# Softmax probabilities copied by DMA and transposed as float32r in whole groups; rotary half copies issued by SyncE

## The chip, the core and the metric

The kernel runs on one core of a Trainium2 chip. Time is device time in microseconds (us) for one execution, the median of several runs. A profile of one execution is read beside it. The engines are PE (TensorE: matmuls, with its weight loads as PEld), DVE (VectorE), ACT (ScalarE), POOL (GpSimd) and SP (SyncE, which only issues DMAs here). Each runs its own queue of instructions in order, and they wait for each other by semaphores.

## The reference

Two layers of a flow-matching backbone over 512 latent tokens and 256 context tokens, model width 1024, in float32. Each layer normalises and modulates its input, projects it into three groups of eight attention heads (width 64) and a gate, attends, and projects back:

```python
hx = rmsnorm(x, norm_w) * (1 + scale[:, None, :]) + shift[:, None, :]
px = split_cols(hx @ w_in)
ya, yca = global_gqa(px[0], px[1], px[2], ...)          # A: all latent and context keys, rotary
yb, ycb = neighbourhood_attn(px[3], px[4], px[5], ...)  # B: 8 x 16 window on a grid, bias, context keys
yc_, ycc = window_gqa(px[6], px[7], px[8], ...)         # C: +-128 tokens, rotary, sink, context keys
ux = jnp.concatenate([ya, yb, yc_], axis=-1) * jax.nn.silu(px[9])
x = x + gate[:, None, :] * (ux @ w_out)
```

Every group is a softmax over scores and a weighted sum of values:

```python
p = softmax_f32(s, v_all.dtype)
return jnp.einsum('bhgqk,bkhd->bqhgd', p, v_all)
```

In the first layer the context tokens go through the same weights and attend to themselves; the second layer computes latent tokens alone.

## The kernel before

**Numbers.** Most matmuls run in float32r, whose precision is not enough alone, so each operand is split into a high part (a rounded copy, made by ACT) and a low part (the rest, by DVE or POOL), and products are summed from two or three such pairs. A weight block is loaded to `ws` by SP (L251 and L497), rounded to `wh` (L242) and subtracted to `wl` (L245).

**Attention.** For a head, `scores` multiplies a tile of 128 queries with the keys into PSUM (`Sbig`); DVE takes the row maximum (`negm`, in B and C with the mask added on the way into `P`); ACT writes the exponentials into an SBUF tile `P` of 128 rows and up to 768 columns, in float32, and sums the rows. `values` needs P with the keys on the partitions, so PE transposes it, 128 x 128 at a time, into a PSUM bank `T` (2 buffers): `turn`, L1031, a matmul in transpose mode with the P block as the stationary operand and the identity as the moving one. The bank is a group: the blocks of two to four query tiles for one key block (B and C), or four blocks of two tiles (A and the context). `pt_copy` splits T into `pth` (ACT) and `ptl` (DVE), and `pv` (L1028) multiplies both with the values `vt` into `Obig`. There are four passes over P per pair of heads in A (two tiles of queries each), two in B and C (four tiles each), and two more for the context queries in the first layer. `o_out` (L1043) then adds the upper and the lower half of `Obig` into `OT`: ACT copies rows 64 to 128 to a scratch tile `otmp`, DVE adds rows 0 to 64 to it.

P has five buffers (`P=5` in CFG, L51).

**Rotary of C.** In `rope_c` (L945) the four 32-row bands of q are swapped by four DMAs of 64 KB from SBUF to SBUF (`tB<-tA`, L958), issued by ACT; POOL multiplies and adds.

**Order.** The program is written as generators that interleave one pair's attention with the next pair's projection. The order that counts is made by a planner, `arrange`: it builds a graph of all instructions, with buffers and PSUM banks, gives each instruction a cost (`Step.cost`) and lays the engines' queues out by list scheduling in several passes; the result is fixed as the order of each engine's queue, SP's included. Its costs are numbers in the code; for PE 108 ns for a float32 transpose, for a DMA 330 ns of SP or 260 of another queue, and then 2550 ns plus the bytes at 395 a ns until it has landed.

Of the kernel before, what the change touches and what calls it, by code (L numbers as in the profile page):

```python
# [20 lines left out]
D = 1024  # L21
# [29 lines left out]
CFG = dict(hp=600, hpf=600, pj=2, T=2, O=1, P=5, qt=5, kt=4, vt=4, gt=3, wh=5, ws=3, pt=3, bm=2, tA=1, OT=1, u=1, tl=1, turns=6, ab="pj", tR=1, map={}, ada=2, h0=300, h1=1000, a0=9, H=2, hr=0, cp="A", cv="A", w0="D", w1="D", w2=(("D", "D"), ("D", "D")), hb="D", ws_="P")  # L51
# [700 lines left out]
def mixers(tc, nc, l, last, p1, ps, const, env):  # L752
# [192 lines left out]
    def rope_c(s, scale, need_ctx, bank):  # L945
# [11 lines left out]
        for b in range(4):  # L957
            nc.scalar.dma_start(sw[b * 32:(b + 1) * 32], q[(b ^ 1) * 32:((b ^ 1) + 1) * 32])  # L958
# [70 lines left out]

    def turn(*args, **kw):  # L1030
        return nc.tensor.transpose(*args, **kw)  # L1031
# [12 lines left out]
    def o_out(O, OT, h, c0, n):  # L1044
        tmp = p1.tile([64, 512], F32, name="otmp", bufs=1)
        nc.scalar.activation(tmp[:, 0:n], O[64:128, 0:n], AF.Copy)  # L1046
        nc.vector.tensor_add(OT[64 * h:64 * h + 64, c0:c0 + n], O[0:64, 0:n], tmp[:, 0:n])  # L1047
# [39 lines left out]
    class CtxUnit(Unit):  # L1087
        def scores(self):
# [11 lines left out]
            self.P = newP()  # L1100
            for t in range(2):
                nc.scalar.activation(self.P[:, t * 256:(t + 1) * 256], S[:, t * 256:(t + 1) * 256], AF.Exp,
                                     bias=self.stat("negm", 4 + t), accum_out=self.stat("sums", 4 + t))
            yield 0.45

        def values(self):
            T = psT()
            for kb in range(2):
                for t in range(2):
                    turn(T[:, (2 * kb + t) * 128:(2 * kb + t + 1) * 128],  # L1110
                                        self.P[:, t * 256 + kb * 128:t * 256 + (kb + 1) * 128], ident)
# [8 lines left out]
    class GlobalUnit(Unit):  # L1120
        def scores(self):
# [8 lines left out]
            for i in self.tiles:  # L1130
# [5 lines left out]
                self.P.append(P)  # L1136
                yield 0

        def values(self):
            O = half_O()  # L1140

            def turns(k2):
                T = psT()
                for k in range(2):
                    for j in range(2):

                        o = ((k2 + k + 2) % 6 if j else k2 + k) * 128
                        turn(T[:, (2 * k + j) * 128:(2 * k + j + 1) * 128], self.P[j][:, o:o + 128], ident)
                return pt_copy(T, 512)

            def sums(k2, pt):
                for k in range(2):
                    pv(O, self.v(k2 + k), pt, k * 256, 0, 256, k2 + k == 0, k2 + k == 5)

            yield from ahead([(lambda k2=k2: turns(k2), lambda pt, k2=k2: sums(k2, pt), 0.45) for k2 in range(0, 6, 2)])
# [4 lines left out]
    class BandUnit(Unit):  # L1160
        def scores(self):
# [3 lines left out]
            for pair in ((1, 2), (0, 3)):  # L1165
# [11 lines left out]
                for i in pair:  # L1177
# [10 lines left out]
                    self.P[i] = P  # L1188
# [20 lines left out]
    class NearUnit(Unit):  # L1209
# [9 lines left out]
        def scores(self):  # L1219
            self.P = {}  # L1220
            for i in (1, 2, 0, 3):
# [22 lines left out]
                self.P[i] = P  # L1244
                yield 0

        def values(self):
            O = psO()
            for n, kb in enumerate((4, 5, 1, 2, 3, 0)):
                qs = [i for i in range(4) if kb in self.PLAN[i][4]]  # L1250
                T = psT()
                for j, i in enumerate(qs):
                    o = self.PLAN[i][4][kb]
                    turn(T[:, j * 128:(j + 1) * 128], self.P[i][:, o:o + 128], ident)
# [276 lines left out]
    def urgent(gen):  # L1531
        while True:
# [12 lines left out]
            T=CFG["T"], spr=2, nw=1, P=CFG["P"], qt=CFG["qt"], kt=CFG["kt"], vt=CFG["vt"], gt=CFG["gt"], negm=2,  # L1545
            bm=CFG["bm"], sums=2, pth=CFG["pt"], ptl=CFG["pt"], rec=2, ssA=2, qd=2, qs=2, ex=2, xr=3, xn0=8, room=9,
# [3 lines left out]
TO_PE, TO_OTHER, FIXED, RATE = 400.0, 150.0, 2550.0, 395.0  # L1550
WAIT = {"PE": 53.0, "POOL": 78.0, "ACT": 36.0, "DVE": 36.0, "SP": 30.0}
# [14 lines left out]
class Step:  # L1566
# [16 lines left out]
    def cost(self):  # L1583
# [6 lines left out]
        self.plain = False  # L1590
        if self.dma:
            b = 4 * outs[0][2][0][1] * size(outs[0][2])
            self.busy = 330.0 if e == "SP" else 260.0
            self.move = 3460.0 if stem(outs[0][0].name) == "bc" else b / RATE
        elif e == "PE":
            n = size(ins[0][2])
            self.exact = ins[0][4] == "float32"
            self.busy = (108.0 if n == 128 else 230.0) if self.exact else max(n / 2.4 + 13.5, 66.0)
            self.last = 272.0 if self.exact else n / 2.4 + 180.0
# [34 lines left out]
class Graph:  # L1634


    def __init__(self, steps, tiles, needed):
# [37 lines left out]
        for a, b in needed:  # L1675
            self.before[at[a]].setdefault(at[b], 0)
        self.users = {name: u for name, u in users.items() if name in tiles and not tiles[name][1]}
# [287 lines left out]
```

## Time and profile before

| | |
|---|---|
| Median of 3 runs | 1178.56 us (1177.38 to 1178.78) |
| The profiled execution | 1178.53 us, its span 1176.3 us, mean granted clock 0.996 |
| Instructions profiled | 21720 |
| DMA | 124.21 MB, mean 106 GB/s |
| Costliest groups on PE | L329 `pj<-wh,hL` 189.2 us, L308 `pj<-hL,wh` 186.4 us, L1031 `T<-ident,P` 177.9 us |

The page gives busy time by engine, the span in slices, DMA queues, the chain of work that ended last, and groups of instructions by line, `out<-in`. Matmuls are pipelined, so their durations overlap; what one costs is read from the distance between starts in the timeline. A group's row ends with the idle time of its engine ahead of it and what ended that.

### The profile page before, as it was taken

The numbers are of one execution on the slowest core, as the hardware profiler recorded it, in microseconds if no ns is written. First come the engines' busy times: TensorE is split into PE (matmuls) and PEld (weight loads), VectorE is DVE, ScalarE is ACT, GpSimd is POOL, SyncE is SP. The second block draws the span as 40 slices with busy tenths as digits, with TensorE's granted clock in tenths as the row PEclk, the third lists the DMA queues.
The fourth block names the chain that finished last, engine by engine and source line by source line (L and its number), as shares of the span: only waits on it lengthen the run. The fifth ranks groups of instructions, "written<-read, shape, count | busy, mean of one in ns | idle before, by whom it ended". The sixth has DMA issues, their size and how long they took to land. (4 is left out here: it accounts for less than half of the span.)

```text
span 1176.3 us, 21720 instructions
## 1 busy us (share of the span) xinstructions
PE 1141.1 (97%) x8016; PEld 1028.0 (87%) x8016; DVE 766.3 (65%) x1548; ACT 697.8 (59%) x1581; POOL 401.7 (34%) x496
## 2 busy tenths in 40 slices
PE   5999999999999999999999999999999999999996
PEld 3799989998898898988788999989988989898885
DVE  5667666665455665657979855676665566668652
ACT  5447555566557666678723634555656677778641
POOL 2442111125445456367300030221235665466001
PEclk9999999999999999999999999999999999999998
DMA  9633222213222222122577432233221121123152
GB/s 359 209 99 99 83 70 95 101 55 112 81 69 96 72 77 86 59 64 91 157 253 265 153 129 88 88 98 98 88 79 60 58 72 53 57 63 108 37 170 72
DMA packets 60825, 124.21 MB, mean 106 GB/s; under 512 B 7216, under 2 KB 13488, under 8 KB 60720
## 3 DMA queue, kind: packets, MB, share of 16 engines
q1 hardware_dynamic: 54768, 111.96, 29.8%
q10 hardware_dynamic: 5952, 10.88, 2.8%
q8 instruction: 63, 1.03, 0.4%
q14 instruction: 42, 0.34, 0.1%
HBM read 109.05 MB, written 11.14 MB: 102 GB/s over the span
## 5 line engine op out<-in xcount | busy, mean ns | idle before, releaser
L1024 DVE TENSOR_TENSOR ptl<-T,pth 128x512 fp32r<-128x512 f32 (+2 forms) x312 | 181.4, 591 | 119.3 <-ACT pth L778 114.7
L778 ACT ACTIVATE pth<-T 128x512 fp32r<-128x512 f32 (+2 forms) x312 | 160.7, 522 | 103.5 <-PE T L1031 93.1
L329 PE MATMUL pj<-wh,hL 128*128 128x256 f32 x896 | 189.2, 289 | 0.2 <-DVE vt L854 0.2
L308 PE MATMUL pj<-hL,wh 128*128 128x512 f32 x544 | 186.4, 405 | 0.0
L1031 PE MATMUL T<-ident,P 128*128 128x128 f32 x1024 | 177.9, 274 | 5.7 <-DVE ptl L1024 2.8
L1028 PE MATMUL Sbig<-kt,qt 128*128 128x256 f32 (+1 forms) x864 | 162.0, 309 | 1.2 <-DVE negm L1240 0.8
L242 ACT ACTIVATE wh<-ws 128x512 fp32r<-128x512 f32 x192 | 120.2, 630 | 67.3 <-PE pj L308 16.2
L1031 PEld LDWEIGHTS T<-ident,P 128*128 128x128 f32 x1024 | 124.8, 140 | 29.3 <-DVE ptl L1024 8.1
L329 PEld LDWEIGHTS pj<-wh,hL 128*128 128x128 f32 x896 | 147.3, 190 | 2.1 <-issue 1.3
L245 POOL TENSOR_TENSOR wl<-ws,wh 128x512 fp32r<-128x512 f32 x76 | 98.4, 1300 | 122.4 <-ACT wh L242 115.6
L1028 PE MATMUL Obig<-ptl,vt 128*128 128x256 f32 (+2 forms) x432 | 131.1, 317 | 1.4 <-DVE ptl L1024 1.4
L1028 PEld LDWEIGHTS Sbig<-kt,qt 128*128 128x128 f32 x864 | 124.8, 189 | 7.8 <-DVE negm L1240 1.4
L1028 PE MATMUL Obig<-pth,vt 128*128 128x256 f32 (+2 forms) x432 | 130.0, 309 | 1.4 <-ACT pth L778 1.2
L329 PE MATMUL pj<-wl,hL 128*128 128x256 f32 x448 | 128.3, 287 | 0.0
L245 DVE TENSOR_TENSOR wl<-ws,wh 128x512 fp32r<-128x512 f32 x116 | 82.5, 721 | 41.7 <-ACT wh L242 31.9
L308 PEld LDWEIGHTS pj<-hL,wh 128*128 128x128 f32 x544 | 97.1, 189 | 13.9 <-ACT wh L242 0.4
L308 PE MATMUL pj<-hL,wl 128*128 128x512 f32 x272 | 109.0, 401 | 0.1
L1028 PEld LDWEIGHTS Obig<-pth,vt 128*128 128x128 f32 x432 | 81.8, 189 | 7.8 <-ACT pth L778 2.0
L1028 PEld LDWEIGHTS Obig<-ptl,vt 128*128 128x128 f32 x432 | 81.6, 189 | 6.6 <-DVE ptl L1024 2.2
L329 PEld LDWEIGHTS pj<-wl,hL 128*128 128x128 f32 x448 | 85.2, 190 | 1.0 <-issue 0.4
L1413 POOL TENSOR_TENSOR bm<-wr,bm 128x192 f32<-128x192 f32 (+1 forms) x48 | 36.6, 789 | 136.5 <-DMA bm<-mskB_dram 73.2
L1047 DVE TENSOR_TENSOR OT<-Obig,otmp 64x512 f32<-64x512 f32 (+1 forms) x88 | 45.1, 512 | 49.2 <-ACT otmp L1046 48.3
(336 smaller groups left out, 2522.5 us busy)
## 6 DMA issues: line engine op xcount, KB each, us to landing
ws<-wf_dram SPq DMA_DIRECT2D x72, 256.0 KB, 2.9
ws<-wt_dram SPq DMA_DIRECT2D x72, 256.0 KB, 2.9
ada<-adaw_dram SPq DMA_DIRECT2D x32, 512.0 KB, 5.5
ws<-wo_dram SPq DMA_DIRECT2D x57, 256.0 KB, 2.9
bm<-mskB_dram SPq DMA_DIRECT2D x16, 576.0 KB, 3.5
dots<-adat_dram SPq DMA_DIRECT2D x16, 256.0 KB, 3.1
dw<-adat_dram SPq DMA_DIRECT2D x8, 512.0 KB, 7.3
u<-u ACTq DMA_DIRECT2D x9, 384.0 KB, 2.5
```

Of the source, the lines that this page charges most:

```text
L242: nc.scalar.activation(hi, src, AF.Copy)
L245: eng.tensor_sub(lo, src, hi.bitcast(F32))
L308: nc.tensor.matmul(p[:, 0:n], a[:, r, :], cols(b[kt], c0, n), start=(i == 0), stop=(i == 23))
L329: nc.tensor.matmul(p[:, t * 256:(t + 1) * 256], tok(a[kt], t2 + t), b[:, r, :], start=(i == 0), stop=(i == 23))
L778: nc.scalar.activation(out, src, AF.Copy)
L1024: nc.vector.tensor_sub(lo[:, 0:n], T[:, 0:n], hi[:, 0:n].bitcast(F32))
L1028: return nc.tensor.matmul(*args, **kw)
L1031: return nc.tensor.transpose(*args, **kw)
L1047: nc.vector.tensor_add(OT[64 * h:64 * h + 64, c0:c0 + n], O[0:64, 0:n], tmp[:, 0:n])
L1413: nc.gpsimd.tensor_add(b, src, b)
```

## The change

- Once ACT has written a P tile, SP copies it by DMA into one or two float32r tiles (`ship`): `R5`, 512 columns, five buffers, and for tiles over 512 columns the rest into `R2`, 256 columns, two buffers. The destination is viewed as float32, so the copy is bit for bit. P's buffers go from five to two.
- P is transposed from these copies as float32r, with the float32r identity (`turn_r`). Other float32 transposes stay.
- The planner gets other costs: SP's issue 430 ns, or the values of `ISSUE`; a float32r transpose 65 ns, and 86 ns once for the matmul behind a run of them. All transposes into one bank get the union of their predecessors (a group starts when all its tiles are there), and once a group has begun, its others go first.
- In A, the key blocks are taken in the order 4, 0, 2 instead of 0, 2, 4; context first.
- The rotary copies are issued by SP instead of ACT.
- `o_out` copies one half straight into its place in `OT` and adds the other in place; the scratch tile goes. `qs` has one buffer instead of two.

```diff
-CFG = dict(..., P=5, ...)
+CFG = dict(..., P=2, R5=5, R2=2, ...)
...
-            qs = p1.tile([128, 4, 64], F32, name="qs", bufs=2)
+            qs = p1.tile([128, 4, 64], F32, name="qs", bufs=1)
...
-            nc.scalar.dma_start(sw[b * 32:(b + 1) * 32], q[(b ^ 1) * 32:((b ^ 1) + 1) * 32])
+            nc.sync.dma_start(sw[b * 32:(b + 1) * 32], q[(b ^ 1) * 32:((b ^ 1) + 1) * 32])
...
+    def ship(P, n, small=(0, 0)):
+        a, b = small
+        big = p1.tile([128, 512], F32R, name="R5", bufs=CFG["R5"])
+        lo, hi = (b, n) if a == 0 else (0, a)
+        parts = [(lo, hi, big)]
+        if b > a:
+            parts.insert(0, (a, b, p1.tile([128, 256], F32R, name="R2", bufs=CFG["R2"])))
+        for c0, c1, r in parts:
+            nc.sync.dma_start(r[:, 0:c1 - c0].bitcast(F32), P[:, c0:c1])
+        return parts
+
+    def turn_r(out, R, o):
+        [src] = [r[:, o - c0:o - c0 + 128] for c0, c1, r in R if c0 <= o < c1]
+        return nc.tensor.transpose(out.bitcast(F32R), src, identr)
...
-        tmp = p1.tile([64, 512], F32, name="otmp", bufs=1)
-        nc.scalar.activation(tmp[:, 0:n], O[64:128, 0:n], AF.Copy)
-        nc.vector.tensor_add(OT[64 * h:64 * h + 64, c0:c0 + n], O[0:64, 0:n], tmp[:, 0:n])
+        o, x = 64 * h, 64 * (1 - h)
+        out = OT[o:o + 64, c0:c0 + n]
+        nc.scalar.activation(out, O[x:x + 64, 0:n], AF.Copy)
+        nc.vector.tensor_add(out, O[o:o + 64, 0:n], out)
...
-                    self.P[i] = P
+                    self.P[i] = ship(P, n, {1: (512, 640), 2: (0, 128)}.get(i, (0, 0)))
...
-                    turn(T[:, j * 128:(j + 1) * 128], self.P[i][:, o:o + 128], ident)
+                    turn_r(T[:, j * 128:(j + 1) * 128], self.P[i], o)
...
+ISSUE = dict(tB=580.0, R5=520.0, R2=520.0, wr=680.0)
...
-            self.busy = 330.0 if e == "SP" else 260.0
+            self.busy = ISSUE.get(stem(outs[0][0].name).split("_")[0], 430.0)
...
-            self.busy = (108.0 if n == 128 else 230.0) if self.exact else max(n / 2.4 + 13.5, 66.0)
+            self.switch = 5.0 if exact else 86.0
+            self.busy = (108.0 if n == 128 else 230.0) if exact else n / 2.4 + (13.5 if n > 128 else 12.0)
...
+            if e == "PE" and prev is not None and prev.turn:
+                same = [x for x in now[e] if steps[x[1]].turn == prev.turn]
```

What this does to the queues, at three places. First PE, in the first pass over P of the first layer (head 0 of B). `T_1127` and `T_1152` are the banks of the two context key blocks, `P_1087`, `P_1105`, `P_1112`, `P_1123` the four query tiles, `pj` a projection. Before:

```order
L1031 MATMUL T_1127<-ident_72,P_1112 128x128
L1031 MATMUL T_1127<-ident_72,P_1087 128x128
L1031 MATMUL T_1127<-ident_72,P_1105 128x128
L1031 MATMUL T_1152<-ident_72,P_1112 128x128
L1031 MATMUL T_1152<-ident_72,P_1087 128x128
L308 MATMUL pj_1082<-hL_754,wl_1079 128x512
L1028 MATMUL Sbig_91<-kt_845,qt_835 128x256 x4
L1031 MATMUL T_1152<-ident_72,P_1105 128x128
L308 MATMUL pj_1203<-hC_242,wh_1072 128x256
L1031 MATMUL T_1127<-ident_72,P_1123 128x128
```

In the change, the same two banks, now `T_1135` and `T_1162`, and the four copies:

```order
L308 MATMUL pj_1312<-hL_622,wh_1308 128x512
L1044 MATMUL T_1135<-identr_77,R5_1120 128x128
L1044 MATMUL T_1135<-identr_77,R5_1098 128x128
L1044 MATMUL T_1135<-identr_77,R5_1110 128x128
L1044 MATMUL T_1135<-identr_77,R5_1133 128x128
L1044 MATMUL T_1162<-identr_77,R5_1120 128x128
L1044 MATMUL T_1162<-identr_77,R5_1098 128x128
L1044 MATMUL T_1162<-identr_77,R5_1110 128x128
L1044 MATMUL T_1162<-identr_77,R5_1133 128x128
L308 MATMUL pj_1312<-hL_624,wh_1308 128x512
```

The two groups stood in pieces among other matmuls; now both stand whole, one behind the other, and later in the projection.

Second SP, where the first layer's first C and A heads are projected and attended. `ws` are weight loads, `ada` blocks of the modulation's weights, `tabx` the rotary tables. Before:

```order
L251 DMA ws<-wf_dram 128x512 x3
L936 DMA tabx_3444<-trigC_dram 128x512
L936 DMA tabx_3446<-trigC_dram 128x512
L251 DMA ws<-wf_dram 128x512 x5
L195 DMA ada<-adaw_dram 128x1024
L251 DMA ws<-wt_dram 128x512
L195 DMA ada<-adaw_dram 128x1024
```

In the change, somewhat later in the same stage (`R` is R5 or R2 by its number of columns):

```order
L1039 DMA R_3599<-P 128x256
L1039 DMA R_3598<-P 128x512
L958 DMA tB<-tA 32x512 x2
L1039 DMA R_3606<-P 128x256
L1039 DMA R_3605<-P 128x512
L958 DMA tB<-tA 32x512 x2
L195 DMA ada<-adaw_dram 128x1024
L251 DMA ws<-wt_dram 128x512
L1039 DMA R_3740<-P 128x256
L1039 DMA R_3739<-P 128x512
L195 DMA ada<-adaw_dram 128x1024
```

Copies of P and the rotary copies now stand between the loads, in one queue with them.

Third ACT, at the same rotary. Before:

```order
L953 ACTIVATE tA<-pj 128x64x8
L1135 ACTIVATE P,sums<-Sbig,negm 128x768
L958 DMA tB<-tA 32x512 x4
L1046 ACTIVATE otmp<-Obig 64x256
L778 ACTIVATE pth<-T 128x512
L242 ACTIVATE wh<-ws 128x512
```

In the change:

```order
L953 ACTIVATE tA<-pj 128x64x8
L1152 ACTIVATE P,sums<-Sbig,negm 128x768
L242 ACTIVATE wh<-ws 128x512
L1063 ACTIVATE OT<-Obig 64x256
L1358 DMA u_7_3616<-u 128x768
```

The four rotary issues are gone from ACT's queue, and the copy out of `Obig` goes to `OT`.

More of the change, by code (lines that the diff above doesn't have):

```diff
@@ L1109, in values @@
                 for t in range(2):
[L1110 to L1111 removed]
+                    turn_r(T[:, (2 * kb + t) * 128:(2 * kb + t + 1) * 128], self.P, t * 256 + kb * 128)
             pt = pt_copy(T, 512)
@@ L1147, in turns @@
                         o = ((k2 + k + 2) % 6 if j else k2 + k) * 128
-                        turn(T[:, (2 * k + j) * 128:(2 * k + j + 1) * 128], self.P[j][:, o:o + 128], ident)
+                        turn_r(T[:, (2 * k + j) * 128:(2 * k + j + 1) * 128], self.P[j], o)
                 return pt_copy(T, 512)
@@ L1152, in sums @@
                 for k in range(2):
-                    pv(O, self.v(k2 + k), pt, k * 256, 0, 256, k2 + k == 0, k2 + k == 5)
-            yield from ahead([(lambda k2=k2: turns(k2), lambda pt, k2=k2: sums(k2, pt), 0.45) for k2 in range(0, 6, 2)])
+                    pv(O, self.v(k2 + k), pt, k * 256, 0, 256, k2 + k == 4, k2 + k == 3)
+            yield from ahead([(lambda k2=k2: turns(k2), lambda pt, k2=k2: sums(k2, pt), 0.45) for k2 in (4, 0, 2)])
             o_out(O, self.OT(), self.h, self.tiles[0] * 128, 256)
@@ L1253, in values @@
                     o = self.PLAN[i][4][kb]
-                    turn(T[:, j * 128:(j + 1) * 128], self.P[i][:, o:o + 128], ident)
+                    turn_r(T[:, j * 128:(j + 1) * 128], self.P[i], o)
                 k = len(qs) * 128
@@ L1544 @@
 CAPS = dict(x0=8, ada=9, x1=8, sq=3, rstd=3, pj=CFG["pj"], ws=CFG["ws"], wh=CFG["wh"], wl=CFG["wh"], hL=16, hC=16,
-            T=CFG["T"], spr=2, nw=1, P=CFG["P"], qt=CFG["qt"], kt=CFG["kt"], vt=CFG["vt"], gt=CFG["gt"], negm=2,
-            bm=CFG["bm"], sums=2, pth=CFG["pt"], ptl=CFG["pt"], rec=2, ssA=2, qd=2, qs=2, ex=2, xr=3, xn0=8, room=9,
+            T=CFG["T"], spr=2, nw=1, P=CFG["P"], R5=CFG["R5"], R2=CFG["R2"], qt=CFG["qt"], kt=CFG["kt"], vt=CFG["vt"], gt=CFG["gt"], negm=2,
+            bm=CFG["bm"], sums=2, pth=CFG["pt"], ptl=CFG["pt"], rec=2, ssA=2, qd=2, qs=1, ex=2, xr=3, xn0=8, room=9,
             xn1=8, rbl=2)
@@ L1596, in cost @@
             n = size(ins[0][2])
-            self.exact = ins[0][4] == "float32"
-            self.busy = (108.0 if n == 128 else 230.0) if self.exact else max(n / 2.4 + 13.5, 66.0)
-            self.last = 272.0 if self.exact else n / 2.4 + 180.0
+            exact = ins[0][4] == "float32"
+            self.turn = outs[0][0].name if stem(ins[0][0].name) in ("ident", "identr") and n == 128 else None
+            self.switch = 5.0 if exact else 86.0
+            self.busy = (108.0 if n == 128 else 230.0) if exact else n / 2.4 + (13.5 if n > 128 else 12.0)
+            self.last = 272.0 if exact else n / 2.4 + 180.0
         else:
@@ L1676, in __init__ @@
             self.before[at[a]].setdefault(at[b], 0)
+        run = []
+        for k in [k for k, s in enumerate(steps) if s.engine == "PE"] + [None]:
+            if run and (k is None or steps[k].turn is None or steps[k].turn != steps[run[0]].turn):
+                whole = {}
+                for i in run:
+                    for j, full in self.before[i].items():
+                        if j < run[0]:
+                            whole[j] = max(full, whole.get(j, 0))
+                for i in run:
+                    for j, full in whole.items():
+                        self.before[i][j] = max(full, self.before[i].get(j, 0))
+                run = []
+            if k is not None and steps[k].turn:
+                run.append(k)
         self.users = {name: u for name, u in users.items() if name in tiles and not tiles[name][1]}
@@ L1715, in run @@
         lanes, pipe = [], 0.0
-        done = 0
+        prev, done = None, 0
         def push(k):
@@ L1734, in run @@
                 heapq.heappush(now[e], (r, k))
+            if e == "PE" and prev is not None and prev.turn:
+                same = [x for x in now[e] if steps[x[1]].turn == prev.turn]
+                if same:
+                    now[e].remove(min(same))
+                    heapq.heapify(now[e])
+                    heapq.heappush(now[e], ((-1e18, 0), min(same)[1]))
             r, k = heapq.heappop(now[e])
@@ L1767, in run @@
                 fin = t + s.last
+                if not s.turn and prev is not None and prev.turn:
+                    busy += prev.switch
+                    fin += prev.switch
+                prev = s
             else:
```

13 lines of the change are left out of this document (7 added, 6 removed).

## The prediction

> **What bounds the kernel now.** I read the page's shares first, then busy time by stage, then PE's own waits.
>
> ```profile
> span 1176.3 us, 21720 instructions
> ...
> PE 1141.1 (97%) x8016; PEld 1028.0 (87%) x8016; DVE 766.3 (65%) x1548; ACT 697.8 (59%) x1581; POOL 401.7 (34%) x496
> ...
> 0.00:60.00 60.00, 46.19 (x347) 32.61 (x348) 37.20 (x100) 31.65 (x72) 20.46 (x23) 1.00 0.78 278
> ...
> 110.00:570.00 460.00, 455.90 (x3395) 417.58 (x3394) 294.93 (x609) 295.23 (x694) 191.96 (x240) 1.00 0.26 83
> 720.00:1115.00 395.00, 391.07 (x2716) 356.02 (x2715) 259.00 (x510) 260.38 (x580) 159.23 (x194) 1.00 0.25 75
> ...
> L1031 PE MATMUL T<-ident,P 128*128 128x128 f32 x1024 | 177.9, 274 | 5.7 <-DVE ptl L1024 2.8 <-DVE u L1333 1.3 <-DVE OT L1326 0.9
> ```
>
> Of the three stretches (start and end, length) the first is the start of the program, the other two the attention of the two layers; the columns are PE, PEld, DVE, ACT, POOL, the granted clock, and the DMA share with its GB/s. In the attention PE is idle for 4.1 and 3.9 us in 855, at the full clock. The next engine, DVE, is about 65% busy. So there the time is PE's issue time, and the 1024 turns of P (the last row), nearly all of them in these two stretches, waited 5.7 us in total. A cheaper turn shortens the kernel almost one for one, as long as nothing else becomes late.
>
> **What a turn costs.** The mean of 274 ns is a pipelined duration, not a cost. I measure from the first turn of a run to the second matmul behind it, and take off one ordinary step (0.12 us behind 256 columns, 0.23 behind 512: the distance of starts between plain matmuls). One run of four float32 turns:
>
> ```profile
> 1016.87 0.28 PE L329 MATMUL pj<-wh,hL 128*128 128x256 f32 x1
> 1016.99 0.60 PE L1031 MATMUL T<-ident,P 128*128 128x128 f32 x4
> 1017.34 0.36 PE L1028 MATMUL Obig<-ptl,vt 128*128 128x256 f32 x1
> 1017.55 0.28 PE L1028 MATMUL Obig<-pth,vt 128*128 128x256 f32 x1
> ```
>
> 1017.55 - 1016.99 - 0.12 = 0.44 us, or 0.11 a turn. The matmul behind the run starts soon, but the one after it is 0.21 away instead of 0.12, so the last turn is not free. The trace has float32r turns as well, those of rotated q and k, in the first row all those of q (minimum, median and longest duration), then runs of four and three:
>
> ```profile
> L879 PE MATMUL T<-identr,qd x80: 222/238/306, 256.7 to 1054.9; 128*128 128x128 f32 x80
> ...
> 992.37 0.39 PE L308 MATMUL pj<-hL,wh 128*128 128x512 f32 x1
> 992.60 0.46 PE L879 MATMUL T<-identr,qd 128*128 128x128 f32 x4
> 992.89 0.47 PE L308 MATMUL pj<-hL,wh 128*128 128x512 f32 x1
> 993.20 0.40 PE L308 MATMUL pj<-hL,wl 128*128 128x512 f32 x1
> ...
> 229.26 0.37 PE L840 MATMUL T<-identr,qd 128*128 128x128 f32 x3
> 229.47 0.35 PE L329 MATMUL pj<-wh,hL 128*128 128x256 f32 x1
> 229.66 0.28 PE L329 MATMUL pj<-wl,hL 128*128 128x256 f32 x1
> ```
>
> Four cost 993.20 - 992.60 - 0.23 = 0.37 us. Three cost 229.66 - 229.26 - 0.12 = 0.28, against 0.33 in float32. The fourth costs 0.09, hardly less than a float32 turn; the gain is in the first turns of a run. For a run of two I take 0.21, extrapolated as 0.28 less one late turn of 0.07 to 0.09, against 0.22. A lone turn then gains nothing, which is why the change has to keep groups whole.
>
> **The sum on PE.** P is turned 1024 times, in 312 groups of one PSUM bank each: 184 of four, 32 of three, 96 of two (counted in the order of either kernel). In the order before, 103 of these groups are broken up among matmuls; since float32 costs 0.11 a turn either way, this did not matter. In the order of the change all 312 are whole. Saved: 184 x 0.075 (between 0.07 and 0.08) = 13.8; 32 x 0.05 = 1.6; 96 x 0.01 = 1.0. The q and k turns are also made whole (11 lone ones before, none after): about 0.6. That is **17 us**. Where two groups adjoin, turns five to eight at 0.09 give again 0.36 for four, so the sum stands.
>
> The Trainium skill, "TensorE: Matmul & The Clock Gate", Part 4: PE-mode transpose, gives about 275 ns for a transpose in a kernel's context. The trace has this as a duration (274), while the starts above lie 0.11 apart. Taken as the cost, with the 0.238 of the float32r form (the median of its 80 records), it would make 1024 x 36 ns = 37 us; I follow the starts.
>
> **What is added: the copy between exponential and turn.** Each P goes through one or two DMAs, 312 in all: 64 tiles of the B heads, 64 of C (32 of them in two parts), 64 of A (all in two), 24 of the context. Nothing here touches PE, but the way from scores to turns gets longer.
>
> ```profile
> L1240 DVE CUSTOM_DVE_ANT_0 P<-Sbig,bm x64: 610/648/694, 87.2 to 870.1; 128x512 f32<-128x512 f32 x32, 128x448 f32<-128x448 f32 x32
> L1242 ACT ACTIVATE P<-P,negm x64: 657/693/738, 88.1 to 871.1; 128x512 f32<-128x512 f32 x32, 128x448 f32<-128x448 f32 x32
> ...
> ws<-wf_dram SPq DMA_DIRECT2D x72, 256.0 KB, 2.9
> tB<-tA ACTq DMA_DIRECT2D x40, 64.0 KB, 2.0
> ...
> L251 SPq DMA_DIRECT2D ws<-wf_dram x72: 327/328/1212, 13.9 to 1019.0; - x72
> ```
>
> Score matmul 0.28, reduction 0.65, exponential 0.69: 1.6 us before the copy. No transfer of 256 KB from SBUF to SBUF is in the trace; it lies between 2.0 (the rotary copies, SBUF to SBUF, a quarter of the bytes) and 2.9 us (weights of the same size, from HBM), and I take 2.6, nearer the equal size. The Trainium skill, "DMA: Bandwidth & Descriptors", Anatomy of one DMA, fits 2.0 us plus bytes at 436 GB/s, by which my estimate would be 2.6 as well; it is fitted on another queue, and no run here shows it. So some 4.2 us are needed (4.5 with 2.9). Counting matmuls in the orders at 0.12 and 0.23 us, from a tile's last score matmul to its first turn PE has at least 2.4 us of other work before, and 2.9 or more for 19 tiles in 20; in the change at least 6.0, and 7.6 for 19 in 20. The slack is therefore 0.8 us at its least before and about 1.5 after, and before it sufficed with 5.7 us of waits. The cover is the interleaved projection and the previous head; without it each group would stand for up to 2.6 us. I charge **1 us** of new waits (range 0 to 17, the second rival below).
>
> The copies add 64 MB (KB: 64 x 256, 32 x 320, 32 x 256, 64 x 384, 24 x 256).
>
> ```profile
> q1 hardware_dynamic: 54768, 111.96, 29.8%
> ```
>
> At 29.8% for 112 MB they take 17% of the span, or 24% of the attention stretches, on top of the 25% shown there: about half busy, so I charge nothing. P itself falls from five buffers to two, but a tile now leaves it when its copy lands, some 4 us after its reduction began. Two buffers so let a tile through every 2 us; the stretches need 216 in 855 us, one in 4. Five and two new buffers then hold what is to be turned.
>
> **What moves, and o_out.** Forty rotary copies leave ACT's queue for SP's:
>
> ```profile
> L958 ACTq DMA_DIRECT2D tB<-tA x40: 514/593/858, 275.8 to 1065.2; - x40
> ...
> 878.97 1.95 DMA tB<-tA
> ...
> L1047 DVE TENSOR_TENSOR OT<-Obig,otmp 64x512 f32<-64x512 f32 (+1 forms) x88 | 45.1, 512 | 49.2 <-ACT otmp L1046 48.3
> ```
>
> That frees 40 x 0.59 = 24 us on ACT, which is 59% busy, and gives SP that plus 312 issues, each between the 0.33 of a weight load on SP and the 0.59 of a rotary copy: 127 to 208 us in all, over a span of 1176. ACT is not the bound, so the 24 us are worth nothing directly; the chain of waits goes through such a copy once, at 879 us, for 1.95 us. I take 0, between a gain of 2 and a loss of 2. The attention sums keep their two operations and only lose the scratch tile with its one buffer; DVE's 49 us of waits there do not reach PE. One buffer fewer for qs delays at most 15 rope steps, on POOL, at 34%: 0. The planner's new numbers reorder the start too; with 14 us of PE idle before 60 us, I allow 2 either way.
>
> The profiled execution took 1178.53 us, 2.2 beyond its span, and the median is 1178.56. So 1178.5 - 17 + 1 = **1163 us** (1162.5).
>
> **The rivals.** *The gain comes back as waits.* Each of the 312 groups now stands behind a DMA and, since it starts only when all its tiles have landed, behind the last of up to four. If every third waits 0.14 us, 14.6 us return: 1177. For it: nothing in the trace shows such a wait, so the slack was never tested. Against it: the slack above.
>
> *Slower: copies stuck on SP.* SP issues in order and stands mostly at waits for a weight buffer:
>
> ```profile
> SPq L251 <- POOL wl L245: 298.5, 52, 21.9
> SPq L251 <- DVE wl L245: 160.7, 58, 12.9
> ```
>
> The last column is the longest. Such a wait, 5.7 us on average behind POOL, costs nothing today, because only further loads are queued behind it. In the change copies of P stand there, and behind them PE. Where POOL runs later than the order assumed, the copy is late by the same amount, PE stops, and nothing makes it up. This costs once a copy is later than the slack of 1.5 to 3 us, and turns the sign at 16 us in all, a quarter of a microsecond for each of the 64 passes over P (16 of B, 16 of C, 32 of A). At twice that, 64 x 0.5 = 32 us: **1195**. Against it: the order puts a load ahead of a copy only where its buffer should be free by then.
>
> *The change doesn't do what it says:* the copied tiles turn at the float32 pace of 0.11. Nothing speaks for it, since the q and k runs use the same identity and instruction. It would give 1178.5 + 1 = 1180.
>
> *More than the sum:* ACT, rid of 24 us of issues and of the scratch buffer, delivers earlier, and PE's 8 us of idle time in the attention and some at the start close: 1163 - 8 = 1155 or a little less.
>
> **How the numbers follow.** The forecast, 1156 to 1172 by its own terms, has 0.62; the waits (1172 to 1181) 0.18; SP, slower, 0.12; no cheaper turn 0.03; more than the sum 0.05. A range from 1155 to 1182 leaves out the slower case and most of the last, 0.17. A measurement of this kernel can tell about 0.2% from no change, or 2.4 us: faster means below 1176.2, slower above 1180.9. Faster: 0.62 + 0.05 + 0.08 of the waits' 0.18 = 0.75. Same: the other 0.10 less a tail of 0.01, and the 0.03, makes 0.12. Slower: 0.12 + 0.01 = 0.13.
>
> **What would show it.** Right: the attention stretches together shorter by 15 to 18 us with the same matmuls, and the projections and output stages as long as before; runs of four turns at 0.37 from starts, and no DMA named R5 or R2 among PE's waits beyond 2 us; issue to landing of a copy from 2.0 to 2.9. Wrong in the copy: waits of PE's turns on R5 in many small pieces, or ACT and DVE held for P's two buffers. Wrong on SP: long PE gaps, each opposite a wait of SP for wl, with a copy just behind. If a turn costs what it did, the distance of starts says so without any wait.

## The result, and the profile after

The changed kernel takes **1171.89 us** (median of 8 runs, 1169.76 to 1177.88), the kernel before beside it 1178.66 (8 runs, 1177.38 to 1179.91): a ratio of 0.995 (95% interval 0.993 to 0.997), or 6 to 7 us. The forecast was 15.5 us. The profiled execution took 1171.95 us, 1.8 beyond its span. The page of the changed kernel, its head, busy time and main DMA queue:

```profile
span 1170.2 us, 22714 instructions
...
PE 1130.1 (97%) x8016; PEld 1015.5 (87%) x8016; DVE 765.4 (65%) x1548; ACT 696.4 (60%) x1581; POOL 406.7 (35%) x496
...
q1 hardware_dynamic: 101616, 181.71, 46.5%
...
L1044 PE MATMUL T<-identr,R 128*128 128x128 f32 x1024 | 126.7, 239 | 10.2 <-DMA R<-P 6.7
```

The turns of P are busy for 126.7 us instead of 177.9. Their idle time is 10.2 us, of which 6.7 ended with a copy. The windows of the changed kernel, in the columns of before:

```profile
0.00:60.00 60.00, 46.60 (x360) 33.68 (x361) 38.25 (x101) 32.78 (x72) 22.22 (x24) 1.00 0.74 266
110.00:570.00 460.00, 451.43 (x3387) 409.90 (x3386) 296.05 (x610) 292.62 (x698) 190.85 (x238) 1.00 0.46 156
720.00:1115.00 395.00, 392.89 (x2780) 359.24 (x2779) 261.47 (x519) 262.99 (x588) 161.71 (x196) 1.00 0.46 153
```

In the first layer's attention PE now stands idle for 8.6 us of 460 (4.1 before), in the second's for 2.1. The DMA share is 0.46, as the forecast had it. A run of four float32r turns in the changed kernel's timeline (start, length, line, operation):

```profile
252.44 0.28 PE L329 MATMUL pj<-wh,hL 128*128 128x256 f32 x1
252.56 0.46 PE L1044 MATMUL T<-identr,R 128*128 128x128 f32 x4
252.85 0.35 PE L329 MATMUL pj<-wh,hL 128*128 128x256 f32 x1
253.04 0.28 PE L329 MATMUL pj<-wl,hL 128*128 128x256 f32 x1
```

253.04 - 252.56 - 0.12 = 0.36 us for four, against 0.44 in float32: the turn has the price of the forecast. So I added up PE's stream from its starts. Each step from one start to the next is charged its undisturbed length (0.119 us behind 256 columns, 0.230 behind 512, 0.1085 between float32 turns, the runs of float32r turns as above); what a step takes beyond that is time lost. In us:

| Kernel | PE undisturbed | lost at the start | lost in layer 1 | lost in layer 2 |
|---|---|---|---|---|
| before | 1108.8 | 13.1 | 19.9 | 13.7 |
| the change | 1090.5 | 11.2 | **35.9** | 14.2 |

The stream is 18.3 us shorter (forecast 17), and **16 us of it are lost again in the first layer**. The rows add up to the time from the first matmul's start to the last one's, 3.8 us less than before. Another 2.6 us of the gain lie behind the last matmul: from its start to the end of the span it is 9.7 us in the kernel before and 7.1 in the change. Two rows of the output projection, by line, show where each layer ends (min/median/max ns, first and last start), of before and then of the change:

```profile
L505 PE MATMUL pj<-hC,kept x24: 283/283/283, 674.0 to 678.2; 128*128 128x256 f32 x24
...
L505 PE MATMUL pj<-hL,wh x64: 389/389/478, 1069.3 to 1153.5; 128*128 128x512 f32 x64
```

```profile
L505 PE MATMUL pj<-hC,kept x24: 283/283/283, 678.2 to 682.4; 128*128 128x256 f32 x24
...
L505 PE MATMUL pj<-hL,wh x64: 388/389/497, 1064.4 to 1148.7; 128*128 128x512 f32 x64
```

The first layer ends 4.2 us later than before; by the end of the second the changed kernel is 4.8 ahead. The copies and the moved rotary copies, by line (SP's issue in ns, minimum, median, maximum; then issue to landing in us):

```profile
L1039 SPq DMA_DIRECT2D R<-P x312: 464/471/1617, 88.2 to 1103.1; - x156
...
DMA to landing us min/median/max: 1.8/2.3/6.7
```

```profile
L958 SPq DMA_DIRECT2D tB<-tA x40: 511/583/1428, 272.4 to 1058.6; - x40
```

The median landing is 2.3 us, and 2.4 for the 216 copies of 256 KB, for which the forecast took 2.6. The tail is longer: of the 312 landings one in ten took over 4.1 us. The dearest stall is one of these. The end of its exponentials in ACT's timeline, and SP's timeline behind it:

```profile
309.44 0.19 ACT L1152 ACTIVATION_READ_ACCUMULATOR P<-Sbig,negm 128x1 f32 x1
```

```profile
308.88 0.56 SPq L195 DMA_DIRECT2D ada<-adaw_dram  x1
309.56 0.37 SPq L251 DMA_DIRECT2D ws<-wf_dram  x1
310.04 0.60 SPq L195 DMA_DIRECT2D ada<-adaw_dram  x1
```

The critical chain behind that (start, length, what it went through) and PE's timeline:

```profile
311.05 6.55 DMA R<-P
317.60 0.04 issue
```

```profile
315.09 0.22 PE L1044 MATMUL T<-identr,R 128*128 128x128 f32 x1
317.64 0.49 PE L1044 MATMUL T<-identr,R 128*128 128x128 f32 x3 [2.33 <-DMA R<-P]
317.93 0.54 PE L1028 MATMUL Sbig<-kt,qt 128*128 128x256 f32 x1
318.27 0.63 PE L308 MATMUL pj<-hL,wl 128*128 128x512 f32 x1
318.70 1.05 PE L308 MATMUL pj<-hL,wh 128*128 128x512 f32 x2
```

The tile is done at 309.63, but SP issues its copy at 311.05, 1.4 us later, behind a weight load and a modulation load (`ada`) in its queue. At that moment two modulation loads of 512 KB and a weight load of 256 KB, issued from 308.88 on, have not landed: 1.25 MB. The copy lands after 6.55 us, 0.34 us behind the last of them, and PE waits for 2.33. (The row at 315.09 is the first of the group's four turns: that a group starts when all its tiles are there is a rule of the planner's order; in the run each turn waits for its own tile.) The windows there:

```profile
312.00:316.00 4.00, 3.31 (x20) 2.73 (x19) 2.22 (x4) 1.32 (x3) 2.88 (x2) 1.00 1.01 261
316.00:318.00 2.00, 0.36 (x4) 0.36 (x4) 0.00 (x0) 0.00 (x0) 0.00 (x0) 0.97 0.15 56
318.00:321.00 3.00, 3.00 (x14) 2.51 (x12) 1.61 (x3) 1.88 (x6) 0.33 (x1) 0.50 0.00 0
```

The DMA engines are full (1.01) just then, though 0.46 busy on average. Behind the stall the granted clock is 0.50 for 3 us: a matmul of 512 columns takes 318.70 - 318.27 = 0.43 us instead of 0.23. That is another 1.5 us.

This is not the whole of the 16 us. I split the sum of lost time at the first matmul of the output projection, L505 (550.9 us in the kernel before, 548.9 in the change); the parts come to within 0.5 us of the table. Ahead of it the first layer loses 14.5 us before and 23.9 in the change; PE's waits on copies are 5.9 us of that. Behind it the layer loses 5.3 and 11.5 us, and there no wait of PE ended with a copy. Windows behind it, of before and then of the change:

```profile
565.00:572.00 7.00, 5.77 (x33) 4.46 (x31) 6.30 (x8) 5.14 (x13) 4.54 (x3) 1.00 0.86 278
572.00:577.00 5.00, 4.09 (x27) 3.80 (x28) 5.00 (x12) 2.08 (x6) 0.00 (x0) 1.00 0.47 141
```

```profile
565.00:572.00 7.00, 4.55 (x24) 3.05 (x23) 5.24 (x9) 5.32 (x12) 4.65 (x4) 1.00 1.01 342
572.00:577.00 5.00, 4.15 (x17) 3.33 (x18) 5.00 (x13) 2.63 (x6) 1.88 (x1) 0.69 0.72 235
```

From 560.15 to 572.85 the changed kernel's critical chain runs over DVE and ACT, with no copy in it. Behind a wait of 1.77 us for DVE's `ptl` the granted clock falls a second time, to a mean of 0.69 over 5 us, which costs another 1.5 us.

### The profile page after: what moved, and what is told of

It is laid out like the page before. It is cut to its first block, busy times and chain, and to the rows that moved or that the text cites. A ratio compares the mean times of both kernels' runs of the same rounds, so it can differ in the third digit from the quotient of the medians.

```text
span 1170.2 us, 22714 instructions
## 1 busy us (share of the span) xinstructions
PE 1130.1 (97%) x8016; PEld 1015.5 (87%) x8016; DVE 765.4 (65%) x1548; ACT 696.4 (60%) x1581; POOL 406.7 (35%) x496
## 4 chain that ended last, share of the span: by engine, by line
PE 81%; DMA 6%; DVE 6%; ACT 4%; issue 2%; POOL 1%; SPq 0%; DVEq 0%; ACTq 0%; POOLq 0%
PE pj L329 18%; PE pj L308 18%; PE Obig L1028 9%; PE Sbig L1028 9%; PE T L1044 6%; PE pj L505 5%; DMA R<-P 4%; PE T L505 3%; PE Sbig L505 3%; PE T L329 2%; PE Sbig L416 1%; PE T L1047 1%; PE Sbig L329 1%; DVE junk L151 1%; PE pj L416 1%
## 5 line engine op out<-in xcount | busy, mean ns | idle before, releaser
L329 PE MATMUL pj<-wh,hL 128*128 128x256 f32 x896 | 184.4, 287 | 0.6 <-DVE kt L906 0.4
L308 PE MATMUL pj<-hL,wh 128*128 128x512 f32 x544 | 183.2, 401 | 0.3 <-DVE qt L894 0.2
L1028 PE MATMUL Sbig<-kt,qt 128*128 128x256 f32 (+1 forms) x864 | 155.7, 306 | 0.5 <-ACT P L1119 0.3
L1044 PEld LDWEIGHTS T<-identr,R 128*128 128x128 f32 x1024 | 112.9, 141 | 33.0 <-DMA R<-P 9.4
L1044 PE MATMUL T<-identr,R 128*128 128x128 f32 x1024 | 126.7, 239 | 10.2 <-DMA R<-P 6.7
L1028 PE MATMUL Obig<-ptl,vt 128*128 128x256 f32 (+2 forms) x432 | 128.6, 312 | 0.2 <-DVE ptl L1024 0.2
L1150 DVE TENSOR_REDUCE negm<-Sbig 128x1 f32<-128x768 f32 x64 | 61.1, 955 | 38.4 <-PE Sbig L1028 22.4
L356 POOL TENSOR_TENSOR rstd<-rstd,mhalf 128x2 f32<-128x2 f32 (+1 forms) x6 | 5.4, 902 | 200.6 <-DVE rstd L354 200.6
```

The lines of the kernel that those rows point to most:

```text
L308: nc.tensor.matmul(p[:, 0:n], a[:, r, :], cols(b[kt], c0, n), start=(i == 0), stop=(i == 23))
L329: nc.tensor.matmul(p[:, t * 256:(t + 1) * 256], tok(a[kt], t2 + t), b[:, r, :], start=(i == 0), stop=(i == 23))
L1028: return nc.tensor.matmul(*args, **kw)
L1044: return nc.tensor.transpose(out.bitcast(F32R), src, identr)
L1150: nc.vector.tensor_reduce(nm, S, axis=AX.X, op=OP.max, negate=True)
```

## The experiments

Gains and losses below are the ratio to the kernel before, run on the same chip, less 1 and times 1178.7 us; the intervals of the ratios are 0.001 to 0.002 to either side, or 1 to 2 us. The theories on where the 16 us of waits came from: **T1**, copies queue behind large loads and land late in the first layer; **T2**, the copy's own latency and P's two buffers tighten the order everywhere; **T3**, the other parts (whole groups, rotary copies, sums, planner) lose the time. After the first runs two were added: **T4**, the waits belong to the one order that the planner found; **T5**, they come with the faster PE, in any order. On the parts that I had put at nothing: **T6**, they move the time themselves; **T7**, it is the luck of an order, since each edit gives another.

**direct**: no copies; ACT writes its exponentials rounded to float32r into tiles that PE turns.

```diff
-        for c0, c1, r in parts:
-            nc.sync.dma_start(r[:, 0:c1 - c0].bitcast(F32), P[:, c0:c1])
-        return parts
+        return [(0, n, P)]
...
-                nc.scalar.activation(P[:, p0:p0 + n], P[:, p0:p0 + n], AF.Exp, bias=nm, scale=-1.0,
+                nc.scalar.activation(R[:, p0:p0 + n], P[:, p0:p0 + n], AF.Exp, bias=nm, scale=-1.0,
```

> The changed kernel without any copy: ACT writes the exponentials rounded to float32r into four tiles of 768 columns, which PE turns as float32r in whole groups; the low part of the probabilities is left out thereby (ptl becomes zero), no other work is. Theory 1 (copies queued behind weight and modulation loads land late, and PE waits in the first layer): the 14 us of first-layer waits go, 1158 to 1164 us. Theory 2 (the copy's own latency and P's two buffers make the order tight everywhere): the same, 1158 to 1164. Theory 3 (whole groups, rotary copies on SP, o_out or the planner's new costs lose the time): no better than the change, 1169 to 1174.

Measured: 1155.17 us, 0.9798 (0.9786 to 0.9811), -23.8 us. PE's stream is as short as in the change (1090.6), and the losses are those of before (13.1, 19.8, 11.3). So the waits come with the copies, and T3 falls as their cause. (The edit also gives the exponentials four tiles of 768 columns, and POOL clears their unused columns by a subtraction instead of a memset.) That it gained more than 17 us was not explained by this run.

**copy_f32**: the copies stay, but hold float32, and the turns are float32 ones.

```diff
-        return nc.tensor.transpose(out.bitcast(F32R), src, identr)
+        return nc.tensor.transpose(out, src, ident)
```

> The changed kernel with float32 copies and float32 turns: copies, groups, order rules stay, only the cheaper turn is undone. If the 17 us of turns are all on the path (every theory that keeps my sum): 1186 to 1191 us. If the waits hide part of the turn cost, since PE would have stood there anyway: 1178 to 1185.

Measured: 1175.87 us, 0.9973 (0.9963 to 0.9982), -3.2 us: below both expectations. Its losses are those of before (11.7, 20.9, 14.0) although copies land as late as in the change (median 2.4, at most 6.5 us). So a late copy alone isn't the cost.

**ada_act** and **noada**: the 16 modulation loads of the first layer's attention are issued by ACT, or left out (their matmuls read a resident tile). **noada_before** is the kernel before without them.

```diff
-            nc.sync.dma_start(st, adaw[k, half])
+            (nc.scalar if k >= KT else nc.sync).dma_start(st, adaw[k, half])
```

```diff
-            ada_next.append((job, ada_load(job, g_["qkv"], "vt", CFG["vt"])))
+            ada_next.append((job, [Old(), Old()]))
```

> The changed kernel with the 16 modulation loads (512 KB each) of the first layer's attention issued by ACT instead of SP, so that copies of P do not stand behind them in SP's DMA queue. Theory 1: copies that took 4 to 6.6 us to land drop to about 3, the two waits of 2 to 2.5 us near 315 and 382 us go, 1164 to 1169 us. Theory 2 and 3: no effect beyond the new order, 1170 to 1174.

> The changed kernel without the 16 modulation loads of the first layer's attention: its matmuls read tiles that lie in SBUF already, so this part of the modulation is left out of the result. Theory 1: as above and a little more, 1162 to 1168 us. Theory 2 and 3: 1170 to 1174, since nothing but these loads is gone.

> The kernel before, with the same 16 modulation loads of the first layer left out (their matmuls read a resident tile). If the loads only hurt the copies of P (T1), the kernel before, which has no such copies, gains nothing from their absence: 1177 to 1179 us. If they cost PE time by themselves: 1170 to 1174 us, and the 7.6 us that their absence was worth to the changed kernel say nothing of the copies.

Measured: ada_act 1171.77 us, 0.9939 (0.9927 to 0.9951), no better than the change. noada 1164.20, 0.9877 (0.9864 to 0.9889), 8.6 us better than the change, with 26.3 us lost in the first layer. noada_before 1179.83, 1.0004 (0.9995 to 1.0013). The loads thus cost the kernel before nothing, and the changed one about 8 us; which engine issues them doesn't matter. In noada's windows at the place of the stall:

```profile
312.00:316.00 4.00, 4.00 (x32) 3.60 (x31) 2.36 (x4) 2.22 (x6) 2.64 (x2) 1.00 0.01 3
316.00:318.00 2.00, 2.00 (x21) 2.00 (x20) 1.23 (x4) 1.76 (x5) 1.22 (x4) 1.00 0.22 88
318.00:321.00 3.00, 3.00 (x28) 3.00 (x27) 1.28 (x3) 2.03 (x5) 3.00 (x5) 1.00 0.09 34
```

The DMA engines are free, PE doesn't stop, and the clock stays at 1.00. Ahead of the output projection noada loses 14.4 us, as the kernel before does (14.5; the change 23.9); behind its start 11.3, as the change does (11.5). So the loads bear on the first part alone. noada has an order of its own, so not all of its 8 us need be the loads' doing.

**copies_act**: the copies of P are issued by ACT.

```diff
-            nc.sync.dma_start(r[:, 0:c1 - c0].bitcast(F32), P[:, c0:c1])
+            nc.scalar.dma_start(r[:, 0:c1 - c0].bitcast(F32), P[:, c0:c1])
```

> The copies of P are issued by ACT, right behind its exponentials, instead of by SP. If the copies are late because they stand behind waits in SP's order: 1160 to 1166 us. If they are late on the DMA engines, which all loads share (T1): 1170 to 1175 us, the landings of R as long as before (75th percentile 3 us or more); ACT, 59% busy, has room for 280 issues of 0.5 us.

Measured: 1179.41 us, 1.0000 (0.9989 to 1.0011), worse than either expectation, with landings as late (75th percentile 3.6 us) and 24.6 us lost in the second layer. SP's queue wasn't what made landings late. That the shared DMA engines are fits this run and ada_act; the Trainium skill, "DMA: Bandwidth & Descriptors", Issuing engines are not separate DMA queues, says that DMAs of any engine run on the same 16 DMA engines, and these two runs agree.

**late1500** and **rate250**: the planner is told that copies land 1.5 us later, or that DMAs move 250 GB/s.

```diff
+                if stem(s.use[-1][0].name).split("_")[0] in ("R5", "R2") or stem(s.use[0][0].name).split("_")[0] in ("R5", "R2"):
+                    fin += 1500.0
```

```diff
-TO_PE, TO_OTHER, FIXED, RATE = 400.0, 150.0, 2550.0, 395.0
+TO_PE, TO_OTHER, FIXED, RATE = 400.0, 150.0, 2550.0, 250.0
```

> The changed kernel, with the planner told that a copy of P lands 1.5 us later than it had assumed; nothing else is edited, and the order puts more work between scores and turns. If it is enough that the slack be longer (T1 with a remedy in the order): 1160 to 1166 us, the first layer's excess 20 to 27 us instead of 36. If a late copy is late by more than any order makes room for, or the two buffers of P tighten the order (T2): 1169 to 1174 us.

> The changed kernel, with the planner told that the DMA engines move 250 GB/s instead of 395, so that every load and every copy lands later in its book-keeping, and it spreads them. If the planner's too fast DMA is what lets bursts form (T4): 1160 to 1167 us, the first layer's excess 20 to 28 us. If any order with these copies pays about the same (T5): 1170 to 1176 us.

Measured: late1500 1196.27 us, 1.0153 (1.0135 to 1.0172); rate250 1181.08, 1.0018 (1.0009 to 1.0026). Both are slower than the change. PE's waits in late1500:

```profile
PE Sbig L1028 <- DVE negm L1200: 4.6, 4, 2.3
...
PE T L1044 <- DMA R<-P: 0.6, 1, 0.6
```

The copies are in time (0.6 us instead of 6.7), but 43.4 and 27.7 us are lost in the two layers, at other waits, and the mean granted clock falls to 0.986. Its trace has six stretches at 0.50 ahead of the last matmuls, 27.3 us together, in which PE is busy for 23.3: some 12 of the lost us are the slower clock. An order patient with the copies was short of work elsewhere; where exactly I have not followed.

**Order against speed.** copy_f32 had late copies without the cost, in another order and with a slower PE. To tell T4 from T5, the planner can be told either price whichever turn is issued, so that the turns of one kernel run in the other's order, row for row on all five engines (True in **r_f32order**, False in **f32_rorder**):

```diff
             exact = ins[0][4] == "float32"
+            if any(stem(u[0].name).split("_")[0] in ("R5", "R2") for u in ins):
+                exact = True
```

> Copies and float32r turns as in the change, but the planner charges these turns the float32 price (0.108 us each), so that every engine keeps the order of copy_f32 (1175.9 us), row for row. If the 16 us of waits belong to the order that the planner found (T4: some copies stand behind bursts of loads, in one order more than in another): 1157 to 1163 us. If they come with the faster PE itself, which reaches the same copies and loads earlier (T5): 1168 to 1173 us, about what the change measured.

> The reverse: float32 turns from the copies, in the order of the change, row for row (the planner charges the float32r price). If the waits belong to the order (T4): 1172 + 17 = 1186 to 1190 us. If they come with the faster PE (T5): 1176 to 1181 us, and the landings of R as long as in the change without PE's waits on them.

| us against before (median) | order of copy_f32 | order of the change |
|---|---|---|
| float32 turns | -3.2 (1175.87) | +6.0 (1184.90) |
| float32r turns | -13.9 (1164.79) | -5.9 (1171.89) |

The intervals are 0.9869 to 0.9895 for r_f32order and 1.0035 to 1.0067 for f32_rorder. Each result lies between the two theories, so both hold in part: in a given order the cheap turns are worth 11 to 12 us, not 18, and the order of the change costs 8 to 9 us more than that of copy_f32, with either turn. About 6 of them are lost behind the start of the first layer's output projection: 11.0 and 11.5 us in the order of the change (float32 and float32r turns) against 5.3 and 5.4 in that of copy_f32, where the kernel before has 5.3. The copies of P are the same in all four, and in the profiled runs no wait of PE there ended with one, so that part is the planner's order. PE's waits on copies say the same, in copy_f32, f32_rorder and r_f32order:

```profile
PE T L1044 <- DMA R<-P: 1.7, 2, 1.1
```

```profile
PE T L1044 <- DMA R<-P: 6.5, 6, 2.1
```

```profile
PE T L1044 <- DMA R<-P: 4.1, 5, 1.5
```

**The other parts**, all of which I had put at nothing. **rest** is the change without copies and cheap turns; **rest_rot_act** is rest with the rotary copies on ACT, **rot_act** and **direct_rot_act** are the same edit of the change and of direct. **plan_only** is the kernel before with the planner's new prices and group rule; **whole_only** has the rule with the old prices. **null_before** and **null_after** have 390 for 395 in the planner's DMA rate, which changes nothing but the order. The edits from the change to rest (its core), of the three rotary kernels, from rest_rot_act to plan_only, and from there to whole_only:

```diff
-            self.P = ship(P, 512)
...
-                    turn_r(T[:, (2 * kb + t) * 128:(2 * kb + t + 1) * 128], self.P, t * 256 + kb * 128)
+                    turn(T[:, (2 * kb + t) * 128:(2 * kb + t + 1) * 128],
+                                        self.P[:, t * 256 + kb * 128:t * 256 + (kb + 1) * 128], ident)
```

```diff
-            nc.sync.dma_start(sw[b * 32:(b + 1) * 32], q[(b ^ 1) * 32:((b ^ 1) + 1) * 32])
+            nc.scalar.dma_start(sw[b * 32:(b + 1) * 32], q[(b ^ 1) * 32:((b ^ 1) + 1) * 32])
```

```diff
-        nc.scalar.activation(out, O[x:x + 64, 0:n], AF.Copy)
-        nc.vector.tensor_add(out, O[o:o + 64, 0:n], out)
+        nc.scalar.activation(tmp[:, 0:n], O[64:128, 0:n], AF.Copy)
+        nc.vector.tensor_add(OT[64 * h:64 * h + 64, c0:c0 + n], O[0:64, 0:n], tmp[:, 0:n])
```

```diff
-            self.busy = ISSUE.get(stem(outs[0][0].name).split("_")[0], 430.0)
+            self.busy = 330.0 if e == "SP" else 260.0
...
-            self.switch = 5.0 if exact else 86.0
-            self.busy = (108.0 if n == 128 else 230.0) if exact else n / 2.4 + (13.5 if n > 128 else 12.0)
+            self.busy = (108.0 if n == 128 else 230.0) if exact else max(n / 2.4 + 13.5, 66.0)
```

> Everything of the change but the copies and the float32r turns: rotary copies on SP, two qs, sums without the scratch tile, the planner's new costs and whole groups; P is turned in float32 straight from its five buffers. If the copies are late behind the loads (T1), this part by itself moves little: 1175 to 1179 us, first layer's excess 19 to 22 us. If whole groups, the rotary copies on SP or the planner's new numbers lose the first layer's time (T3): 1182 to 1190 us.

> The kernel rest (1173.6 us: all of the change but copies and float32r turns), with the rotary copies issued by ACT as before. If the 5 us that rest gained come from ACT's 24 us of issues, which I had put at nothing: back to 1177 to 1179 us. If they come from the sums without a scratch tile and the new order: 1172 to 1175 us.

> The changed kernel with the 40 rotary copies issued by ACT as before. If their place behind waits and copies on SP costs what rest and rest_rot_act differ by (6 us): 1164 to 1168 us. If the copies of P set the end, and the rotary copies' place does not matter beside them: 1170 to 1174 us.

> The kernel direct (exponentials written as float32r, no copies: 1155.2 us; the low part of the probabilities is left out) with the rotary copies issued by ACT. If their place on SP costs 6 us whatever stands beside it: 1148 to 1151 us. If it costs what an order's luck does: 1153 to 1157 us.

> The kernel before with the planner's new prices and whole groups alone: rest_rot_act (1167.7 us) with the sums through their scratch tile again. If the planner makes the 11 us: 1166 to 1170 us. If the sums without a scratch tile make them: 1175 to 1179 us.

> The kernel before with the planner's rule that keeps the turns of a group together, and the old prices. If the rule makes the 10 us of plan_only: 1168 to 1171 us. If the prices make them: 1176 to 1180 us.

> The kernel before, with the planner told 390 GB/s instead of 395: the same work in a slightly other order. It measures what an order by itself is worth. If an order's luck is about 1 us (T6: the parts themselves move the time): 1177 to 1180 us. If it is some 5 us (T7): anything from 1173 to 1185, outside 1177 to 1180.

> The changed kernel with the same 390 instead of 395. If the first layer's 16 us of waits are the luck of one order (T7): 1163 to 1168 or 1176 to 1182 us, with the first layer's excess moved by as much. If an order that the planner finds with these copies always pays about the same: 1170 to 1174 us.

| Kernel | median us | ratio (95% interval) | us against before |
|---|---|---|---|
| null_before | 1176.16 | 0.9974 (0.9963 to 0.9985) | -3.1 |
| null_after | 1173.78 | 0.9952 (0.9939 to 0.9965) | -5.7 |
| whole_only | 1183.18 | 1.0034 (1.0021 to 1.0046) | +4.0 |
| plan_only | 1169.00 | 0.9913 (0.9900 to 0.9925) | -10.3 |
| rest_rot_act | 1167.72 | 0.9904 (0.9891 to 0.9917) | -11.3 |
| rest | 1173.60 | 0.9954 (0.9941 to 0.9966) | -5.4 |
| rot_act | 1170.57 | 0.9925 (0.9911 to 0.9940) | -8.8 |
| direct_rot_act | 1156.76 | 0.9802 (0.9788 to 0.9815) | -23.3 |

rest and rest_rot_act came out below both of their expectations, whole_only above both, and null_before (1176.16) outside the 1177 to 1180 that small luck allowed. In the two null kernels an order's luck was worth 0.2 us in the changed kernel and 3.1 in the one before, less than the larger steps. But two tries don't bound it: the same operations in the two orders of the table above differ by 8 to 9 us. So T6 is likelier than T7 for the planner's step, and neither is shown. The planner alone gains 10.3 us; its rule alone loses 4.0, so with the rule in place **the new prices make 14 us**, by the one order that they gave. Rows of plan_only's output projection:

```profile
L505 PE MATMUL pj<-hC,kept x24: 282/283/284, 671.1 to 675.3; 128*128 128x256 f32 x24
...
L505 PE MATMUL pj<-hL,wh x64: 387/390/478, 1061.0 to 1145.1; 128*128 128x512 f32 x64
```

It is 2.9 us ahead of before at the end of the first layer and 8.4 near the end of the second. Its lost time is 11.4, 19.2 and 9.6 us, that of whole_only 15.4, 24.8 and 12.6. And 2.6 us of plan_only's gain lie behind the last matmul, as in the change: from its start to the span's end it takes 7.1 us, 9.7 in before and 10.2 in whole_only. One of the old prices was plainly off: 260 ns for an ACT issue that took 593 for each of 40 rotary copies. Which price does it wasn't tried apart. The rotary copies' move to SP cost 5.9 us without copies of P (rest against rest_rot_act), 2.9 in the change, and nothing in direct: it is no fixed price. rot_act came out where the rotary copies' place was not to matter, direct_rot_act where an order's luck was to explain it.

## Why the prediction was right in sign and wrong in size

Every kernel has an order of its own, so the steps below hold the luck of orders too, and each is good to about 2 us by its ratios. Along one path, in us:

| Step | forecast | measured | between |
|---|---|---|---|
| planner's prices and whole groups | 0 (±2) | -10.3 | before, plan_only |
| sums without scratch tile | 0 | -1.0 | plan_only, rest_rot_act |
| rotary copies on SP | 0 (±2) | +5.9 | rest_rot_act, rest |
| float32r turns (with one qs, other P tiles, A's key order) | -17 | -18.4 | rest, direct |
| copies of P | +1 (0 to 17) | **+17.9** | direct, the change |
| sum | -16 | -5.9 | |

- **The sum on PE** held. Four turns cost 0.36 to 0.37 us, the stream is 18.3 us shorter, and without copies that came through on the clock as 18.4. In a given order with the copies it is 11 to 12.
- **The failed step is the slack**: "The slack is therefore 0.8 us at its least before and about 1.5 after", and so "I charge **1 us** of new waits". It set the order's distance against a typical copy of 2.6 us. The typical copy was faster (2.4 for the same 256 KB), but one in ten took over 4.1 us and the slowest 6.7. It also let a copy start with the end of its exponentials; the one at the dearest stall was issued 1.4 us later. In place of the 1 us the copies cost 17.9, from direct to the change. The rival that the gain comes back as waits is what happened, at the upper end of my range, but not as "every third waits 0.14 us": seven waits of the turns make 6.7 us, the longest 2.3. The rest of the 16 us was lost around them: two stretches of slower clock are 3 us, and about 6 us lie in the output projection's part, with the order and without a wait on a copy. Not all of it is accounted for.
- **"About half busy, so I charge nothing"** failed with it. The share is 0.46, and the engines were full for 4 us where it mattered. The 25% before was of loads, and none of PE's waits there ended with one; a copy that is wanted at once lands behind them. Without these loads the changed kernel was 8 us faster, the one before was not.
- **The edits put at nothing** were the other error. Of the planner's numbers I wrote "I allow 2 either way": they brought 10.3 us; along this path the other steps sum to +4.4. The 6 us gained are not those I predicted: cheap turns and copies together came to nothing (-18.4 + 17.9), so that the sign came out right was luck.
- **Copies stuck on SP** didn't happen as told. SP's waits in the change, the queue's own:

```profile
SPq L251 <- DVE wl L245: 91.5, 50, 9.3
SPq L1039 <- PE T L1044: 79.6, 53, 10.6
SPq L1039 <- ACT P L1152: 56.8, 24, 8.4
SPq L251 <- POOL wl L245: 55.3, 34, 10.2
```

SP now stands at copies, for a free R buffer or for exponentials, and behind POOL's `wl` for 55.3 us instead of 298.5. Issued by ACT, the copies took as long to land. At the dearest stall, though, the copy was issued 1.4 us after its exponentials, behind two loads in SP's queue. Whether the weights queued behind a waiting copy cost something wasn't tried.
- **No cheaper turn** falls with the run of four. Why a faster PE loses 7 us more to the same copies in the same order, while loads and copies are the same, stays open: less time to the same landings is the likely reason, but no run shows it by itself.

## What to carry to other kernels

Set the slack of a new transfer against its slow landings, one in ten, at the places where loads of half a megabyte are issued just ahead of it, and not against a typical landing and a mean DMA share. Where a planner's prices change, charge that as an edit of its own and run it alone: here it was worth more than the edit that the change is named for. And where a result could be the luck of an order, hold the order fixed and swap the operation alone, as r_f32order and f32_rorder do; the fastest kernel with the copies that does all the work, r_f32order, came out of that.

## What the runs showed of the hardware

- The granted clock fell to 0.50 for 3 us behind a stall of only 2.33 us. The Trainium skill, "TensorE: Matmul & The Clock Gate", What's actually happening, has the clock halved after at least one idle window of about 3.4 us; here a shorter gap did, as the row 318.00:321.00 shows. At this place the stall cost 1.5 us more than its own length. The row 572.00:577.00 shows the same behind a wait of 1.77 us. The gap's length alone doesn't decide it: in f32_rorder the wait of 2.1 us on a copy, which ends at 320.1, left the clock at 1.00 until 326, and so did a wait of 1.7 us in the kernel before, which ends at 572.9, until 590.
- A 256 KB copy from SBUF to SBUF landed in 2.4 us at the median (216 copies; all 312, from 64 to 256 KB, 1.8 to 6.7), and SP took 0.47 us to issue it, against 0.33 for a weight load.
